# A decoder trunk in fp32r matmuls: rows of matmuls behind the last store, and the order in the last k tile

## The chip, the core and the metric

The kernel runs on one NeuronCore of a Trainium2 chip. The metric is device time in microseconds, from the first to the last instruction of one execution with what lies around it. Before the change two runs took 2795.05 and 2796.88 us (median 2795.97). The core has five engines with queues of their own: TensorE (PE; its weight loads are PEld), VectorE (DVE), ScalarE (ACT), GpSimd (POOL) and SyncE (SP), which issues most DMAs.

## The reference

256 tokens of width 2048 pass through two layers. Each layer is a token mixer and a SwiGLU feed-forward, each wrapped in RMS norms and a residual. The first mixer is HGRN2 beside Mamba-2, the second a causal Conformer convolution.

```
h = x
for layer in range(DEPTH):                       # 2
    u = rms_norm(h, mix_pre_g[layer])
    m = hgrn2_mamba2_mixer(u, ...) if layer % 2 == 0 else conformer_conv_module(u, ...)
    h = h + rms_norm(m, mix_post_g[layer])
    u = rms_norm(h, ffn_pre_g[layer])
    h = h + rms_norm(swiglu(u, w_gate, w_up, w_down), ffn_post_g[layer])
return h
```

All data are float32. Nearly all arithmetic lies in the products with weights (w_in, w_out, w1, w2, gate, up, down).

## The kernel before

Activations lie transposed: `h` is a tile of 128 partitions x 16 k tiles x 256 tokens. A product with weights is done in fp32r, the type in which TensorE takes a rounded float32. To keep accuracy each operand is split into a high part (rounded) and a low part (the rest), and three of the four products are summed: high x high, high x low and low x high.

`weights` (line 138) loads 4 k tiles of a block of 256 columns by a DMA of SyncE, ScalarE makes the high part (line 144), VectorE or GpSimd the low part (line 145). The result lies in one of 4 buffers `whl`. `gemm` (line 178) goes over k in steps of 4 tiles, over the blocks, over the two halves `f` of a block, and over the k tiles, and calls `mm` (line 151) for each. `mm` issues two matmuls: `main`, whose moving operand has 512 columns (high and low part of the activations, side by side), and `cross`, with 256 (low part of the weights times high part of the activations), which is added into the second half of the same PSUM bank. In the last k tile of a half block `cross` comes first:

```
steps = [(ps, *main, first, last), (ps[:, 256:512], *cross, False, False)]
for o, l, r, st, sp in (steps[::-1] if last else steps):
```

`evac` (line 242) then takes a block out of PSUM: ScalarE copies the second halves (line 248), VectorE adds the first halves (line 252). `mm_one` (line 159) does the same product in three matmuls of 256 columns; the last block of each `project` uses it (line 161). `dt_rows` (line 542) issues its pairs of 512 and 256 columns on lines of its own, 552 and 555. Column sums for the norms (`colsum`, line 259) are fp32 matmuls of one column, which stand as two rows each in the trace.

The order of the instructions on each engine is set by a scheduler that simulates the program; `urgent`, `first` and `soon` give priorities, and `pin` keeps an instruction in the order in which the code issues it. The order within a queue is fixed before the run; engines wait for each other by semaphores.

`run` (line 492) goes through mixer, feed-forward, Conformer, feed-forward. The last `residual` calls `output` (line 336): it multiplies the last projection by the norm's factor, adds it to `h` and stores `h` in blocks of two k tiles, on SyncE's or ScalarE's queue. For blocks 3 and 4 (`PEF`) TensorE adds (lines 345 and 375) and ScalarE copies the sum into `h` (line 377). The last store is block 4's, on ScalarE's queue. With it the program ends.

Of the kernel before, what the change touches and what calls it, by code (L numbers as in the profile page):

```python
# [11 lines left out]
F32R = mybir.dt.float32r  # L12
# [4 lines left out]
P = 128  # L17
# [5 lines left out]
CK = 4  # L23
# [41 lines left out]
class Trunk:  # L65
# [84 lines left out]

    def mm(self, ps, main, cross, first, last, pin=False):
        nc = self.nc
        steps = [(ps, *main, first, last), (ps[:, 256:512], *cross, False, False)]
        for o, l, r, st, sp in (steps[::-1] if last else steps):
            self.last = nc.tensor.matmul(o, lhsT=l, rhs=r, start=st, stop=sp, skip_group_check=True)  # L155
            if pin:
                self.pin(self.last)
# [334 lines left out]
    def run(self, parts):  # L492
        us = self.residual(None, None, "mix_pre" if parts[0] in "mc" else "ffn_pre", 16 * (parts[0] == "c"), parts[0] == "c")
        layer = 0
        for n, p in enumerate(parts):
            nxt = parts[n + 1:n + 2]
            if p == "m":
                ms, rp = self.mixer(us)
            elif p == "c":
                ms, rp = self.conformer(us)  # L500
            else:
                ms, rp = self.ffn(layer, us)
                layer += 1
            pre = {"": None, "f": "ffn_pre"}.get(nxt, "mix_pre")
            us = self.residual(ms, rp, pre, layer * KT, nxt == "c")

# [674 lines left out]
```

## Time and profile before

| | |
|---|---|
| median of two runs | 2795.97 us |
| profiled execution: time | 2796.62 us |
| profiled execution: span, first to last instruction | 2794.9 us |
| TensorE busy | 2722.8 us, 97% |
| weight loads (PEld) busy | 2378.2 us, 85% |
| VectorE / ScalarE / GpSimd busy | 64% / 53% / 17% |
| mean granted TensorE clock | 0.986 |
| chain that ended last | TensorE 66%, VectorE 7% |

Times in the views are microseconds from the start of the span. "Busy" of TensorE is modelled: matmuls overlap, so the busy time of one is longer than its distance to the next. The granted clock is a share of full speed, 1.00 being 2.4 GHz and 0.50 being 1.2 GHz. A few matmul records can be missing from a trace.

### The profile page before, as it was taken

The numbers are of one execution on the slowest core, as the hardware profiler recorded it, in microseconds if no ns is written. First come the engines' busy times: TensorE is split into PE (matmuls) and PEld (weight loads), VectorE is DVE, ScalarE is ACT, GpSimd is POOL, SyncE is SP. The second block draws the span as 40 slices with busy tenths as digits, with TensorE's granted clock in tenths as the row PEclk, the third lists the DMA queues.
The fourth block names the chain that finished last, engine by engine and source line by source line (L and its number), as shares of the span: only waits on it lengthen the run. The fifth ranks groups of instructions, "written<-read, shape, count | busy, mean of one in ns | idle before, by whom it ended". The sixth has DMA issues, their size and how long they took to land.

```text
span 2794.9 us, 41558 instructions
## 1 busy us (share of the span) xinstructions
PE 2722.8 (97%) x16362; PEld 2378.2 (85%) x16362; DVE 1786.4 (64%) x2372; ACT 1470.2 (53%) x1978; POOL 483.4 (17%) x308
## 2 busy tenths in 40 slices
PE   7999999999999999999999999999999999999998
PEld 6888888887788888888888888987878888888887
DVE  6876777887645655555544458996575555554444
ACT  6676775666544544444444445555554444444443
POOL 2221321111100100000000016981110000000001
PEclk9999999999999999999999999999999999999999
DMA  6454455555565555555566644542545555556663
GB/s 216 155 173 157 154 168 159 171 175 169 177 186 162 160 188 188 185 186 188 185 186 188 188 152 155 182 150 79 163 160 187 187 185 186 188 185 186 187 188 121
DMA packets 134020, 482.41 MB, mean 173 GB/s; under 512 B 14880, under 2 KB 15424, under 8 KB 133824
## 3 DMA queue, kind: packets, MB, share of 16 engines
q1 hardware_dynamic: 132528, 476.41, 54.6%
q8 instruction: 128, 2.10, 0.3%
q10 hardware_dynamic: 1296, 3.35, 0.3%
q14 instruction: 68, 0.56, 0.1%
HBM read 477.57 MB, written 2.13 MB: 172 GB/s over the span
## 4 chain that ended last, share of the span: by engine, by line
PE 66%; DVE 7%; issue 1%; ACT 1%; ACTq 0%; DVEq 0%
PE g L155 57%; PE g L161 7%; DVE pc L911 3%; DVE u L288 1%; DVE whl L145 1%; DVE m L426 0%; DVE h L429 0%; DVE ca L977 0%; PE ss L262 0%; ACT whl L144 0%; DVE m L351 0%; PE g L921 0%; DVE h L415 0%; PE pc L921 0%; PE rb L275 0%
## 5 line engine op out<-in xcount | busy, mean ns | idle before, releaser
L145 DVE TENSOR_TENSOR whl<-raw,whl 128x1024 fp32r<-128x1024 f32 x846 | 1060.3, 1255 | 902.1 <-ACT whl L144 896.3
L155 PE MATMUL g<-u,whl 128*128 128x256 f32 (+1 forms) x8448 | 1524.4, 342 | 28.5 <-DVE u L288 26.9
L144 ACT CAST whl<-raw 128x1024 fp32r<-128x1024 f32 x898 | 939.0, 1048 | 1086.0 <-PE g L155 869.4
L155 PEld LDWEIGHTS g<-u,whl 128*128 128x128 f32 x8448 | 1303.8, 190 | 234.6 <-DVE u L288 31.4
L155 PE MATMUL g<-hid,whl 128*128 128x512 f32 (+1 forms) x2464 | 434.7, 339 | 0.6 <-DVE m L252 0.6
L155 PEld LDWEIGHTS g<-hid,whl 128*128 128x128 f32 x2464 | 377.3, 188 | 57.9 <-PE g L155 1.1
L480 POOL TENSOR_TENSOR sg<-sg,rpre 128x512 f32<-128x512 f32 x44 | 77.6, 1763 | 874.9 <-ACT sg L479 874.9
L161 PE MATMUL g<-u,whl 128*128 128x256 f32 x1536 | 193.2, 289 | 9.2 <-DVE u L288 6.1
L161 PEld LDWEIGHTS g<-u,whl 128*128 128x128 f32 x1536 | 190.8, 197 | 11.1 <-DVE u L288 7.7
L911 DVE SCALAR_TENSOR_TENSOR pc<-ca,dw,pc 128x240 f32<-128x240 f32 (+29 forms) x414 | 158.2, 461 | 0.4
L311 POOL TENSOR_TENSOR acc<-acc,sq 128x512 f32<-128x512 f32 x24 | 37.9, 1579 | 645.1 <-ACT sq L310 645.1
L145 POOL TENSOR_TENSOR whl<-raw,whl 128x1024 fp32r<-128x1024 f32 x52 | 126.0, 2442 | 37.1 <-ACT whl L144 34.8
L155 PE MATMUL g<-whl,u 128*128 128x256 f32 (+1 forms) x512 | 95.8, 343 | 1.2 <-DVE f L252 1.2
L155 PEld LDWEIGHTS g<-whl,u 128*128 128x128 f32 x512 | 78.8, 188 | 13.3 <-issue 1.5
L155 PE MATMUL g<-cx,whl 128*128 128x512 f32 x448 | 84.3, 352 | 4.3 <-DVE cx L1060 2.8
L248 ACT COPY ev<-g 128x512 f32<-128x512 f32 x153 | 88.1, 576 | 0.0
L791 POOL TENSOR_TENSOR e<-e,cbm 128x384 f32<-128x384 f32 x32 | 45.6, 1444 | 235.6 <-ACT e L789 188.3
L155 PEld LDWEIGHTS g<-cx,whl 128*128 128x128 f32 x448 | 72.1, 198 | 16.5 <-DVE cx L1060 3.5
L155 PE MATMUL g<-mixb,whl 128*128 128x512 f32 (+1 forms) x448 | 81.1, 340 | 1.5 <-DVE mixb L132 1.5
L155 PE MATMUL g<-mixa,whl 128*128 128x512 f32 x448 | 80.3, 339 | 1.5 <-DVE m L252 1.5
L155 PEld LDWEIGHTS g<-mixb,whl 128*128 128x128 f32 x448 | 68.7, 188 | 12.6 <-DVE mixb L132 2.2
L155 PEld LDWEIGHTS g<-mixa,whl 128*128 128x128 f32 x448 | 68.9, 188 | 12.1 <-issue 2.1
(278 smaller groups left out, 1851.7 us busy)
## 6 DMA issues: line engine op xcount, KB each, us to landing
raw<-ffn_gu SPq DMA_DIRECT2D x352, 512.0 KB, 3.5
raw<-w_in SPq DMA_DIRECT2D x208, 512.0 KB, 4.5
raw<-ffn_d SPq DMA_DIRECT2D x176, 512.0 KB, 3.6
raw<-w SPq DMA_DIRECT2D x96, 512.0 KB, 3.6
raw<-w_out SPq DMA_DIRECT2D x64, 512.0 KB, 3.8
row<-csd SPq DMA_DIRECT2D x16, 256.0 KB, 5.6
h<-x ACTq DMA_DIRECT2D x4, 512.0 KB, 9.0
raw<-w_dt SPq DMA_DIRECT2D x2, 512.0 KB, 4.2
```

The lines of the kernel that those rows point to most:

```text
L144: nc.scalar.copy(hl[:, :n, 0], raw[:, :n])
L145: (lo or nc.vector).tensor_tensor(hl[:, :n, 1], raw[:, :n], hl[:, :n, 0].bitcast(F32), ALU.subtract)
L155: self.last = nc.tensor.matmul(o, lhsT=l, rhs=r, start=st, stop=sp, skip_group_check=True)
L161: self.last = self.nc.tensor.matmul(ps[f] if banks else ps[:, f], lhsT=hl[:, wi, f * P:(f + 1) * P], rhs=x[:, xi], start=k == 0 and n == 0 ...
L248: nc.scalar.copy(ev[:, sl], ps[:, sl, 256:512])
L288: pin(self.nc.vector.scalar_tensor_tensor(u[:, 1], x, sc, u[:, 0].bitcast(F32), op0=ALU.mult, op1=ALU.subtract))
L311: nc.gpsimd.tensor_tensor(acc, acc, sq, ALU.add)
L480: nc.gpsimd.tensor_tensor(sg, sg, self.bc2(r), ALU.mult)
L791: G.tensor_tensor(e, e, cb, ALU.mult)
L911: x = V.scalar_tensor_tensor(pc[f][:, s:T], a[:, f, 0:T - s], tap(2 * i + f, s), pc[f][:, s:T], op0=ALU.mult, op1=ALU.add)
```

## The change

It has two parts. In `mm` the last k tile now issues `main` first and `cross` second, as all others do; the flag that ends the accumulation moves to `cross`. Behind the last `residual` a new function `trials` is called. ScalarE copies parts of the final `h` into three `whl` buffers and eight activation tiles; the copies read blocks 4 to 7 of `h`. Then TensorE runs matmuls on these, all fp32r but for `tiny`, each with start and stop set, into two PSUM tiles that nothing reads: `pairs` as in `mm` (with other moving operands, other banks or other weights as options), `grouped` and `swapped` (the same pairs in other orders), `wide` (three of 512 columns with activations as the stationary operand), `ones` (256 columns), `halves` (512 columns) and single matmuls of 1 to 512 columns in between (`kick`, `tiny`). Three passes go through all forms, four passes through `pairs` behind kicks of each length.

```diff
@@ -150,8 +150,7 @@
 
     def mm(self, ps, main, cross, first, last, pin=False):
         nc = self.nc
-        steps = [(ps, *main, first, last), (ps[:, 256:512], *cross, False, False)]
-        for o, l, r, st, sp in (steps[::-1] if last else steps):
+        for o, l, r, st, sp in ((ps, *main, first, False), (ps[:, 256:512], *cross, False, last)):
             self.last = nc.tensor.matmul(o, lhsT=l, rhs=r, start=st, stop=sp, skip_group_check=True)
             if pin:
                 self.pin(self.last)
@@ -503,6 +502,127 @@
                 layer += 1
             pre = {"": None, "f": "ffn_pre"}.get(nxt, "mix_pre")
             us = self.residual(ms, rp, pre, layer * KT, nxt == "c")
+        self.trials()
+
+    def trials(self):
+        nc = self.nc
+        S = nc.scalar
+        flat = lambda a: a.rearrange("p a b -> p (a b)")
+        hw = self.h.rearrange("p a b -> p (a b)")
+        ws = []
+        for n in range(3):
+            w = self.whl.tile([P, CK, 2, 256], F32R, tag="whl", name=f"pw{n}")
+            wf = w.rearrange("p a b c -> p (a b c)")
+            self.pin(S.copy(wf, hw[:, 2048:4096]))
+            ws.append(w)
+        xs = []
+        for n in range(8):
+            x = self.A(F32R, name="px")
+            self.pin(S.copy(flat(x), hw[:, 3584 - 64 * n:4096 - 64 * n]))
+            xs.append(x)
+        xf = [flat(x) for x in xs]
+        ps = [self.ps_gemm() for _ in range(2)]
+        o = [p[:, j] for p in ps for j in range(2)]
+        st = {"k": 0}
+
+        def mm(out, l, r):
+            self.pin(nc.tensor.matmul(out, lhsT=l, rhs=r, start=True, stop=True, skip_group_check=True))
+
+        def places(n):
+            k0 = st["k"]
+            st["k"] += n
+            for j in range(k0, k0 + n):
+                i, f, t = j % 4, j // 4 % 2, j // 8 % 2
+                yield i, f, slice(f * P, (f + 1) * P), ws[t], j % 8
+
+        def pairs(n, gap=False, banks=False, other=False):
+            for i, f, s, w, k in places(n):
+                b = o[k % 4] if banks else o[f]
+                r = ws[2][:, 0:2, 0] if gap else xf[k]
+                lo = ws[2][:, i, 1, s] if other else w[:, i, 1, s]
+                mm(b, w[:, i, 0, s], r)
+                mm(b[:, 256:512], lo, ws[2][:, 0, 0] if gap else xs[k][:, 0])
+
+        def grouped(n, g):
+            pl = list(places(n))
+            for q in range(0, n, g):
+                for i, f, s, w, k in pl[q:q + g]:
+                    mm(o[f], w[:, i, 0, s], xf[k])
+                for i, f, s, w, k in pl[q:q + g]:
+                    mm(o[f][:, 256:512], w[:, i, 1, s], xs[k][:, 0])
+
+        def swapped(n):
+            for i, f, s, w, k in places(n):
+                m = [(o[f], w[:, i, 0, s], xf[k]), (o[f][:, 256:512], w[:, i, 1, s], xs[k][:, 0])]
+                for a in (m[::-1] if k % 2 else m):
+                    mm(*a)
+
+        def wide(n, gap=False, banks=False):
+            for i, f, s, w, k in places(n):
+                b = [o[(3 * k + j) % 4] for j in range(3)] if banks else [o[f]] * 3
+                hi = ws[2][:, 0:2, 0] if gap else flat(w[:, i])
+                lo = ws[2][:, 0:2, 1] if gap else flat(w[:, (i + 1) % 4])
+                mm(b[0], xs[k][:, 0, s], hi)
+                mm(b[1], xs[k][:, 0, s], lo)
+                mm(b[2], xs[k][:, 1, s], hi)
+
+        def ones(n, gap=False):
+            for i, f, s, w, k in places(n):
+                r = ws[2][:, 0:2, 0, 0:P] if gap else xs[k][:, 0]
+                mm(o[f][:, 0:256], w[:, i, 0, s], r)
+
+        def halves(n, gap=False):
+            for i, f, s, w, k in places(n):
+                mm(o[f], w[:, i, 0, s], ws[2][:, 0:2, 0] if gap else xf[k])
+
+        def kick(n):
+            mm(o[0][:, 0:n], ws[0][:, 0, 0, 0:P], xf[0][:, 0:n])
+
+        def tiny():
+            mm(o[0][:, 0:1], self.ident, self.ones[:, 0:1])
+
+        halves(24)
+        for _ in range(3):
+            pairs(16)
+            kick(128)
+            pairs(16, gap=True)
+            kick(384)
+            pairs(16, banks=True)
+            kick(256)
+            pairs(16, other=True)
+            tiny()
+            grouped(16, 2)
+            kick(128)
+            grouped(16, 4)
+            kick(320)
+            swapped(16)
+            kick(64)
+            wide(8)
+            kick(192)
+            wide(8, gap=True)
+            kick(448)
+            wide(8, banks=True)
+            kick(128)
+            ones(16, gap=True)
+            kick(256)
+            halves(16)
+            kick(192)
+            halves(16, gap=True)
+        for _ in range(4):
+            for n in (64, 128, 192, 256, 320, 384, 448, 512):
+                kick(n)
+                pairs(11)
+            kick(128)
+            kick(128)
+            pairs(11)
+            kick(256)
+            kick(256)
+            pairs(11)
+            kick(512)
+            kick(512)
+            pairs(11)
+            tiny()
+            pairs(11)
```

On TensorE, at the last k tile of a half block of the first products (`g` is the PSUM tile, `u` the activations, `whl` the weights). Before:

```order
L155 MATMUL g_195<-u_141,whl_325 128x512
L155 MATMUL g_195<-u_141,whl_325 128x256
L155 MATMUL g_195<-u_144,whl_325 128x256
L155 MATMUL g_195<-u_144,whl_325 128x512
L155 MATMUL g_195<-u_135,whl_325 128x512
L155 MATMUL g_195<-u_135,whl_325 128x256
```

And now:

```order
L154 MATMUL g_195<-u_141,whl_325 128x512
L154 MATMUL g_195<-u_141,whl_325 128x256
L154 MATMUL g_195<-u_144,whl_325 128x512
L154 MATMUL g_195<-u_144,whl_325 128x256
L154 MATMUL g_195<-u_135,whl_325 128x512
L154 MATMUL g_195<-u_135,whl_325 128x256
```

The two matmuls of the k tile `u_144` have changed places. There are 332 such places; one cast of ScalarE, one subtraction of GpSimd and a few matmuls near the norms also stand a place or two elsewhere.

On ScalarE, the end of the program as it is now (`out` and `h` are the output and the residual stream, `pw` and `px` the copies for `trials`):

```order
L357 DMA out<-h 128x512
L376 COPY h<-g_24318 128x512
L357 DMA out<-h 128x512
L516 CAST pw0_24351<-h_86 128x2048
L516 CAST pw1_24353<-h_86 128x2048
L516 CAST pw2_24355<-h_86 128x2048
L521 CAST px2994_24357<-h_86 128x512
L521 CAST px2995_24359<-h_86 128x512
```

Eleven copies stand behind the last store's issue, where the program ended before.

On TensorE, what stands behind the last matmul of `output` (line 374 now):

```order
L374 MATMUL g_24318<-m_23480,ident 128x512
L529 MATMUL g_24373<-px_24357,pw_24351 128x512
L529 MATMUL g_24373<-px_24359,pw_24351 128x512
L529 MATMUL g_24373<-px_24361,pw_24351 128x512
L529 MATMUL g_24373<-px_24363,pw_24351 128x512
L529 MATMUL g_24373<-px_24365,pw_24351 128x512
L529 MATMUL g_24373<-px_24367,pw_24351 128x512
L529 MATMUL g_24373<-px_24369,pw_24351 128x512
L529 MATMUL g_24373<-px_24371,pw_24351 128x512
```

These are the first eight of `halves(24)`; each waits for its own copy by ScalarE, the later ones for nothing but TensorE's own order.

## Rows read from the trace of the kernel before

**Rows 1.** The page's part 1: busy time, share of the span, instructions.

```profile
span 2794.9 us, 41558 instructions
PE 2722.8 (97%) x16362; PEld 2378.2 (85%) x16362; DVE 1786.4 (64%) x2372; ACT 1470.2 (53%) x1978; POOL 483.4 (17%) x308
```

**Rows 2.** Timeline of ScalarE's last instructions: start, us, engine, line, operation.

```profile
2791.35 0.59 ACT L377 COPY h<-g 128x512 f32<-128x512 f32 x1 [2.33 <-PE g L375]
2791.97 0.34 ACTq L358 DMA_DIRECT2D out<-h  x1
```

**Rows 3.** Stretches at the end: us, PE busy (matmuls), granted clock, DMA share, GB/s.

```profile
2786.00:2792.00 6.00, 4.11 (x4) 0.54 0.46 177
2792.00:2795.00 3.00, 0.00 (x0) 0.50 0.44 171
```

**Rows 4.** Timeline of TensorE in `dt_rows`: 16 pairs of 512 and 256 columns.

```profile
62.70 0.40 PE L552 MATMUL g<-u,whl 128*128 128x512 f32 x1
62.93 0.28 PE L555 MATMUL g<-u,whl 128*128 128x256 f32 x1
63.04 0.40 PE L552 MATMUL g<-u,whl 128*128 128x512 f32 x1
63.27 0.28 PE L555 MATMUL g<-u,whl 128*128 128x256 f32 x1
63.39 0.40 PE L552 MATMUL g<-u,whl 128*128 128x512 f32 x1
63.63 0.28 PE L555 MATMUL g<-u,whl 128*128 128x256 f32 x1
63.75 0.40 PE L552 MATMUL g<-u,whl 128*128 128x512 f32 x1
...
67.99 0.40 PE L552 MATMUL g<-u,whl 128*128 128x512 f32 x1
```

**Rows 5.** Dense stretches (columns as rows 3), and the timeline of the last one.

```profile
2200.00:2300.00 100.00, 100.00 (x568) 1.00 0.58 186
2754.00:2777.00 23.00, 23.00 (x193) 1.00 0.23 69
...
2753.84 23.64 PE L161 MATMUL g<-hid,whl 128*128 128x256 f32 x195
```

**Rows 6.** Timeline of TensorE at two calls of `colsum`, four matmuls.

```profile
2753.03 0.95 PE L262 MATMUL ss<-ones,acc 128*128 128x1 f32 x8
```

**Rows 7.** Groups of ScalarE by shape: count, busy us, mean ns, idle before.

```profile
L144 ACT CAST whl<-raw 128x1024 fp32r<-128x1024 f32 x898 | 939.0, 1048 | 1086.0 <-PE g L155 869.4 <-issue 135.6 <-PE g L161 54.6
L248 ACT COPY ev<-g 128x512 f32<-128x512 f32 x153 | 88.1, 576 | 0.0
```

**Rows 8.** Timeline of TensorE where it resumes behind idle times.

```profile
899.90 14.01 PE L155 MATMUL g<-u,whl 128*128 128x512 f32 x64 [2.98 <-DVE u L288]
...
920.10 10.89 PE L155 MATMUL g<-u,whl 128*128 128x512 f32 x44 [2.13 <-DVE u L288]
...
2038.36 8.35 PE L155 MATMUL g<-u,whl 128*128 128x512 f32 x35 [2.36 <-DVE u L288]
```

**Rows 9.** Stretches around these places, columns as in rows 3.

```profile
898.60:905.40 6.80, 5.50 (x17) 0.52 0.23 77
905.40:915.60 10.20, 8.52 (x48) 0.99 0.12 40
915.70:925.80 10.10, 7.71 (x21) 0.51 0.50 167
925.90:936.00 10.10, 10.10 (x62) 0.99 0.47 149
2035.20:2042.00 6.80, 4.43 (x12) 0.52 0.41 139
2042.00:2060.00 18.00, 17.72 (x105) 0.99 0.53 165
```

## The prediction

> **What bounds the kernel now.** I read the page's totals first: TensorE is busy 97% of a span of 2794.9 us [rows 1], so what is added to it, with nothing beside it that could shrink, is added to the time. The reader should then look at the tail, because the change puts its work there. The timeline ends with a copy of ScalarE from PSUM into `h` and the issue of the last store at 2791.97 us, done 0.34 us later [rows 2]; TensorE has nothing to do from there on, and the granted clock has fallen to 0.50, the 1.2 GHz level [rows 3]. The third reading is the price of the added instructions, from stages that run the same shapes in the same type (fp32r, 128 rows). The best is the stage of `dt_rows`, whose two matmuls stand on lines of their own, so that the timeline doesn't merge them [rows 4]. A "mean ns of one" is no price: matmuls overlap, so I take the distance from one start to the next.
>
> **The prices.** In [rows 4] the 512-column matmul starts at 62.70 and, fifteen pairs on, at 67.99: 5.29/15 = 0.353 us for a pair of 512 and 256 columns. The page of a long stage agrees: 568 matmuls in 100 us are 0.176 each [rows 5]. Within the pair, the 256 starts 0.23 to 0.24 after the 512 (mean 0.236) and the next 512 starts 0.11 to 0.12 after that. A run of 256-column matmuls alone, in the last block, takes 23.64/195 = 0.121 each [rows 5]. So a matmul costs 0.461 ns a column (0.236/512), and short ones don't fall below some floor: eight rows of one column take 0.95 us, 0.119 each [rows 6].
>
> **First part: trials().** Counting the calls gives 2208 matmuls of 871,751 columns:
> 864 pairs: seven lots of 16 (pairs four times, grouped twice, swapped) in each of 3 passes are 336; twelve lots of 11 in each of 4 passes are 528. At 0.353: 305.0 us.
> 336 matmuls of 512 columns that stand alone: 24 at the start, and in each of 3 passes 72 of `wide` and 32 of `halves`. At 0.236: 79.3 us. No row shows 512 behind 512 for long; pair minus 256 alone (0.353 - 0.121 = 0.232) says 78.0, so this is worth 1.3 us either way.
> 48 of 256 columns (`ones`): 48 x 0.121 = 5.8 us.
> 89 kicks: 51 of 256 columns and more, 18,816 columns in all, 8.7 us at 0.461 ns; 38 shorter ones at the floor of 0.119, 4.5 us.
> 7 times `tiny`, fp32 with one column, two rows in the trace each (four such matmuls of `colsum` show eight [rows 6]): 7 x 0.24 = 1.7 us.
> Sum: 305.0 + 79.3 + 5.8 + 8.7 + 4.5 + 1.7 = 405.0 us.
>
> The start is set by ScalarE, which must make the operands first. It is free at 2791.97 + 0.34 = 2792.3. Its copies take 0.576 us for 128x512 and 1.048 for 128x1024 [rows 7], so 0.472 more for each further 512: about 1.99 for 128x2048. Three of these are 5.97 us and eight of 128x512 are 4.61; with 0.03 between two of them the first `px` is there at 2799.0 and the last at 2803.2. The first eight matmuls wait for one `px` each and are shorter than its copy even at half clock (0.47), so they hide under it. The other 16 of the first 24 then run free. The clock is low when they begin. How long it stays low: TensorE starts again at 899.90, 920.10 and 2038.36 [rows 8] and the stretches at 0.5 end at 905.4, 925.8 and 2042.0 [rows 9], that is 3.6 to 5.7 us after the work came back. Counted from 2799.0, it rises between 2802.6 and 2804.7. I take 2804.5: 1.3 us at half clock does about 3 of the 16, the other 13 take 3.1 us, and the passes begin at 2803.2 + 4.4 = 2807.6. With all 16 cold it would be 3 us more, with none 0.6 less.
>
> What remains is the sum without the first 24 (5.7 us): 399.3. End: 2807.6 + 399.3 + 0.2 (a 256-column matmul lasts 0.28 us, 0.16 more than its step) = 3207.1. The last stores are long landed by then and hide. The profiled execution took 2796.62 for its span of 2794.9, so 1.7 lie around the span: 3208.8. Its time is 0.65 over the median of 2795.97 that the forecast is set against: **3208 us**.
>
> **Second part: the order in the last k tile.** 332 half blocks now issue 512, 256 where they issued 256, 512. The columns, the instructions and the waits' number are the same. Nobody waits for the middle of a half block: the copy out of PSUM waits for the last instruction, which is now the 256 one. Steps differ by at most 0.01 from one place to the next in [rows 4]; 332 x 0.01 bounds it at 3.3 us in either direction, and I take nothing. The other moves that the schedule shows (one cast of ScalarE and one subtraction of GpSimd a place later, two short matmuls of a norm earlier) neither add nor remove work; a late one of about 1 us each is their bound.
>
> **A rule against this sum.** Each 512 in [rows 4] takes 0.236 us, each 256 in [rows 5] 0.121, at granted clock 1.00. The Trainium skill, "TensorE: Matmul & The Clock Gate", section "Back-to-back issue gap", says that a warm stream needs N/2.4 + 2.5 ns for N columns, which would be 0.216 and 0.109. By that the whole sum is an estimate of 871,751/2400 + 2208 x 0.0025 = 369 us in place of 405; the rows are about a tenth dearer, and they decide the sum. It is a rival below.
>
> **Rivals.**
> (a) *Cheap trials.* The tenth above one column a tick (2.4 GHz: 512 columns 0.213) comes from something that the trials lack, such as the weights' transfers, the other engines' reads, or adding into PSUM (all trial matmuls overwrite). One column a tick is 871,751/2400 = 363 us, 42 less: 3166. By the rule of the Trainium skill named above it would be 3172. Against it: the last block's 256s step at 0.121 with DMA at 0.23 and most engines idle, the same as elsewhere [rows 5]. 7%.
> (b) *Some forms are dearer.* The "gap" lots read the moving operand in two runs of 256 that lie apart, which no matmul here does. Per pass they are 16 pairs, 24 + 16 of 512 and 16 of 256: 5.6 + 9.4 + 1.9 = 17.0 us, 51 in three passes. At double price the time is 3259; at a third more, 3225. Likewise `wide`, with 216 matmuls. 11%.
> (c) *The trials hardly run.* This one ends on the other side, not slower. No instruction reads the PSUM tiles that they write; if whatever turns the program into what the chip runs drops them, only the copies are left: 2803.8 + 1.7 = 2805, no change. It decides once fewer than some 250 of the 2208 remain, 250 x 0.18 us being 45 us beside the 9 of the copies. Against it: the built program's TensorE list holds them all, behind line 375's. 3%.
> (d) *The clock stays low* through the trials: twice 405, about 3610. In stages as dense as these it is 1.00 [rows 5]. 1%.
>
> **Chances and range.** The forecast's case has 78%. Its own unknowns are the price of a pair (1% is 4 us), the start (-0.6 to +3), the order (3) and the moved steps (2): 3197 to 3221. To hold 8 in 10 beside the rivals, and since some lots may each be a tenth off without being (a) or (b), I take 3183 to 3236. What a measurement here can tell from no change is 2%, 56 us: slower 97%, within 2% 2%, faster 1%, the last two from (c).
>
> **What would show it.** In the profile after: a span near 3207; the first trial matmul at 2799; the clock rising some 2 to 6 us later and staying at 1.00; stretches of `pairs` at 0.353 a pair whatever kick stands ahead; the same step of 0.23 to 0.24 in `wide` and `halves`; the main program's last store at 2792 within 5 us. Wrong would be: pairs at 0.32 (a); gap lots that take longer than their neighbours (b); no rows of the trials (c).

## The result, and the profile after

The changed kernel takes 3178.35 us (two runs, 3177.28 and 3179.42) against 2795.97: 1.1367 of the time before, 95% interval 1.1344 to 1.139. Slower, as forecast, but 4.7 us under the range and 30 under the number. The profiled execution took 3177.28 us for a span of 3175.6.

The end of the main program comes first. The timeline after, at the same instructions as [rows 2], and then the first of `trials` (start, us, engine, line, operation, idle before):

```profile
2766.91 0.59 ACT L376 COPY h<-g 128x512 f32<-128x512 f32 x1 [2.29 <-PE g L374]
2767.53 0.34 ACTq L357 DMA_DIRECT2D out<-h  x1
2767.96 5.50 ACT L516 CAST pw<-h 128x2048 fp32r<-128x2048 f32 x3 [0.47 <-ACT h L376]
2773.36 4.25 ACT L521 CAST px<-h 128x512 fp32r<-128x512 f32 x8
...
2774.03 13.63 PE L529 MATMUL g<-px,pw 128*128 128x512 f32 x57 [7.16 <-ACT px L521]
```

The last store is issued at 2767.53 where it was at 2791.97: the main program, whose instructions are the same but for 332 exchanged pairs, became 24.4 us shorter. Where that went shows in counts of matmuls per 100 us. After, columns as in [rows 3]:

```profile
1000.00:1100.00 100.00, 100.00 (x579) 1.00 0.61 190
1500.00:1600.00 100.00, 100.00 (x567) 1.00 0.63 185
2200.00:2300.00 100.00, 100.00 (x579) 1.00 0.62 190
2600.00:2700.00 100.00, 100.00 (x567) 1.00 0.63 187
```

Before, the stretch from 2200 held 568 [rows 5]. It lies in the second feed-forward's gate and up blocks, and now holds 579; the stretches from 1500 and 2600, in the down projections, hold 567, no more than before:

```profile
1500.00:1600.00 100.00, 100.00 (x568) 1.00 0.63 185
2600.00:2700.00 100.00, 100.00 (x571) 1.00 0.64 189
```

The same two speeds stand in `dt_rows`, now on lines 672 and 675:

```profile
61.03 0.39 PE L672 MATMUL g<-u,whl 128*128 128x512 f32 x1
61.26 0.28 PE L675 MATMUL g<-u,whl 128*128 128x256 f32 x1
61.38 0.39 PE L672 MATMUL g<-u,whl 128*128 128x512 f32 x1
61.61 0.28 PE L675 MATMUL g<-u,whl 128*128 128x256 f32 x1
...
66.23 0.39 PE L672 MATMUL g<-u,whl 128*128 128x512 f32 x1
```

From 61.03 to 66.23 are fifteen pairs: 0.3467 us each, where [rows 4] had 0.3527. The starts of all pairs in the trace say it to the nanosecond. A long stream of pairs runs in a **rhythm**. The slow one repeats every three pairs (steps of 233, 117, 241, 120, 236, 113 ns: 1060 for three, 353.3 a pair). The fast one takes 346.7 a pair (230 and 117, or 232, 118, 231, 112, 233, 117, 231, 113). Each gate and up stage has 1408 pairs; the last 1335 run on without a wait. Before, all but the first 20 or so of these were in the slow rhythm, some 1316 in either stage. After, all 1335 are in the fast one.

The page's totals after, beside [rows 1]:

```profile
span 3175.6 us, 46001 instructions
PE 3099.9 (98%) x18577; PEld 2723.7 (86%) x18577; DVE 1785.8 (56%) x2372; ACT 1483.5 (47%) x1989; POOL 483.4 (15%) x308
```

TensorE has 2215 rows more: the 2208 matmuls of `trials`, and a second row for each of the seven `tiny`.

### The profile page after: what moved, and what is told of

It is laid out like the page before. It is cut to its first block, busy times and chain, and to the rows that moved or that the text cites. A ratio compares the mean times of both kernels' runs of the same rounds, so it can differ in the third digit from the quotient of the medians.

```text
span 3175.6 us, 46001 instructions
## 1 busy us (share of the span) xinstructions
PE 3099.9 (98%) x18577; PEld 2723.7 (86%) x18577; DVE 1785.8 (56%) x2372; ACT 1483.5 (47%) x1989; POOL 483.4 (15%) x308
## 4 chain that ended last, share of the span: by engine, by line
PE 70%; DVE 6%; ACT 1%; issue 1%; ACTq 0%; DVEq 0%
PE g L154 50%; PE g L529 13%; PE g L160 6%; DVE pc L1031 2%; DVE u L287 1%; DVE whl L145 1%; DVE m L425 0%; DVE h L428 0%; DVE ca L1097 0%; PE ss L261 0%; ACT whl L144 0%; DVE m L350 0%; PE g L1041 0%; DVE h L414 0%; PE pc L1041 0%
## 5 line engine op out<-in xcount | busy, mean ns | idle before, releaser
L154 PE MATMUL g<-u,whl 128*128 128x512 f32 (+1 forms) x8448 | 1503.7, 339 | 27.4 <-DVE u L287 27.3
L529 PE MATMUL g<-px,pw 128*128 128x256 f32 (+3 forms) x1793 | 320.2, 339 | 7.2 <-ACT px L521 7.2
L529 PEld LDWEIGHTS g<-px,pw 128*128 128x128 f32 x1793 | 276.6, 189 | 49.3 <-ACT px L521 10.4
L154 PE MATMUL g<-whl,u 128*128 128x512 f32 (+1 forms) x512 | 95.2, 341 | 0.6 <-DVE f L251 0.6
L154 PE MATMUL g<-mixb,whl 128*128 128x512 f32 x448 | 81.7, 342 | 1.6 <-DVE mixb L132 1.6
```

The costliest lines, as they stand in the source:

```text
L529: self.pin(nc.tensor.matmul(out, lhsT=l, rhs=r, start=True, stop=True, skip_group_check=True))
```

## The experiments

Three theories of the 24.4 us were on the table. *Rhythm*: an exchange at a half block's end throws the stream into the slow rhythm, where it stays. *Local*: each reversed end costs 24.4/332 = 74 ns where it stands. *Schedule*: the code behind the last store moved the main program.

### One part at a time

e1_order_only has no `trials`; e2_trials_only has the old order. Their edits are the two halves of the change; e1_order_only's, against the changed kernel, is this line:

```diff
-        self.trials()
```

> The changed kernel without trials(): only the order in the last k tile differs from the kernel before. Three theories of where 24.4 us of the main program went. Rhythm: the pair stream of TensorE runs in one of several repeating rhythms, of 353.3 or 346.7 ns a pair, and the reversed half-block end throws it into the slow one; without it 2771.5 us. Local: each of the 332 reversed ends costs 74 ns where it stands; also 2771.5. Schedule: the code behind the store moved the main program's schedule, and the order is worth nothing; 2796.

> The old order in the last k tile, with trials() behind the last store. The trials and their copies took 407.9 us in the changed kernel (3178.35 - 2770.45 of e1_order_only). If the two parts of the change add up, this is the kernel before (2793.5 to 2796.0) and 408: 3201.5 to 3204, with gate and up pairs at 353.3 ns. If the trials' presence is what moved the main program, 3178.

Measured: e1_order_only 2770.45 us (2767.34 to 2770.68) against 2793.52 before it, ratio 0.9916 (0.9901 to 0.9931). e2_trials_only 3201.12 against 2795.35, 1.1452 (1.1419 to 1.1485). The parts add up: the order alone gives 23.1 us back, the trials alone cost 405.8. *Schedule* falls. In a stretch of the first gate and up stage, e1_order_only, then e2_trials_only:

```profile
1000.00:1100.00 100.00, 100.00 (x579) 1.00 0.53 190
```

```profile
1000.00:1100.00 100.00, 100.00 (x568) 1.00 0.60 187
```

The rate goes with the order, whatever stands behind the store.

### The order or the flag

e9_flag_on_main exchanges nothing but leaves the flag that ends the accumulation on the 512-column matmul.

```diff
-        for o, l, r, st, sp in ((ps, *main, first, False), (ps[:, 256:512], *cross, False, last)):
+        for o, l, r, st, sp in ((ps, *main, first, last), (ps[:, 256:512], *cross, False, False)):
```

> As e1_order_only (512 columns first, 256 second, everywhere), but the flag that ends the accumulation stays on the 512-column matmul, as it was before the change. If the order of the two matters: 2767 to 2778 and gate and up pairs at 346.7. If the place of the flag was what slowed the kernel before: 2796 and 353.3.

2774.42 us, 0.9931 (0.9913 to 0.9949); both gate and up stages are fast:

```profile
1000.00:1100.00 100.00, 100.00 (x579) 1.00 0.53 190
2200.00:2300.00 100.00, 100.00 (x579) 1.00 0.53 190
```

e1_again, the same order with the flag on the 256-column matmul, took 2773.92 beside it. The flag has no part in it.

### One place instead of 332

e3_one_block_reversed puts the old order back in one block of the first feed-forward:

```diff
+            self.flip = i == 1 and layer == 0
             ps = pss[0] if i == 0 else self.gemm(wgu, g[:1], us)[0]
+            self.flip = False
```

> As e1_order_only, but one block of 256 columns (i = 1, gate, first feed-forward) has the old reversed order in its two half-block ends. Rhythm: the two ends switch the stream to 353.3 ns a pair and it stays there for what is left of the gate and up blocks, 42 blocks x 32 pairs x 6.67 ns = 9.0 us over e1_order_only; the second feed-forward stays at 346.7. Local: 2 x 74 ns = 0.15 us over e1_order_only, and 346.7 in both.

2777.76 us, 7.3 over e1_order_only in the same batch (*rhythm* forecast 9.0). Times of whole programs vary by several us from one execution to the next, so the rates of the stages decide. The stretches of the first and of the second feed-forward:

```profile
1000.00:1100.00 100.00, 100.00 (x567) 1.00 0.52 187
2200.00:2300.00 100.00, 100.00 (x579) 1.00 0.53 190
```

Two exchanged places slow all 1485 pairs behind them, from 941 to 1466 us. *Local* allowed 0.15 us. The steps around the first of the two, from the starts in the trace (columns of the matmul: step to the next, ns):

```
... 512:230 256:117 512:230 256:116 | 256:119 512:232 | 512:231 256:113 512:233 256:117 512:241 256:120 ...
```

The two exchanged matmuls themselves cost 351 ns, as a pair should. Behind them the fast rhythm (230, 117) has become the slow one (233, 117, 241, 120).

The kernel before shows the same switch. The long runs of pairs of its two gate and up stages start fast and turn slow at their first exchanged places, at 944.38 and 2062.30 us, and the steps around the first of these are those shown above. So does its first down projection, at 1501.16, the first exchanged place behind the wait at 1472.

An exchange is not a one-way switch, though. In e2_trials_only, which has the old order, the first down projection is slow, turns fast at the exchange at 1499.76 us, and slow again at the one at 1530.29:

```profile
1471.00:1496.00 25.00, 25.00 (x143) 1.00 0.62 187
1502.00:1527.00 25.00, 25.00 (x146) 1.00 0.65 191
1533.00:1558.00 25.00, 25.00 (x143) 1.00 0.63 187
```

And where a second exchange stands four pairs behind one that led to the fast rhythm, the stream can stay fast (before, at 79.28 us, for one). In the two gate and up stages of before and of e2_trials_only no exchange leads back.

e7_one_end_and_reset is finer: one exchanged place in all, at i = 4, and four short matmuls at i = 13.

```diff
+                        if self.reset and k == 0 and f == 1:
+                            for _ in range(4):
+                                self.nc.tensor.matmul(ps[:, f, 0:1], lhsT=self.ident, rhs=self.ones[:, 0:1], ...)
...
+            self.flip = i == 4 and layer == 0
+            self.reset = i == (13 if layer == 0 else 4)
```

> As e1_order_only; in the first feed-forward one single half-block end is reversed (i = 4, gate, f = 0) and four 1-column fp32 matmuls (overwritten) stand between the half blocks of i = 13, gate; in the second feed-forward only the four matmuls stand, at i = 4. Rhythm: first feed-forward 346.7 ns a pair up to i = 4, 353.3 from there to i = 13, 346.7 behind it: 9 x 64 pairs x 6.67 ns = 3.8 us and 0.5 for the four matmuls; second feed-forward 346.7 throughout, 0.5 us more. Sum 4.8 over e1_order_only. Local: 0.07 + 1.0 us, 346.7 throughout.

Stretches before the exchange, behind it (two), behind the four matmuls, and in the second feed-forward:

```profile
950.00:1000.00 50.00, 50.00 (x291) 1.00 0.59 191
1050.00:1100.00 50.00, 50.00 (x284) 1.00 0.57 184
1150.00:1200.00 50.00, 50.00 (x285) 1.00 0.58 185
1250.00:1300.00 50.00, 50.00 (x290) 1.00 0.59 190
2200.00:2250.00 50.00, 50.00 (x290) 1.00 0.59 189
```

Fast, slow from 1012 to 1206 us (547 pairs), fast again, as *rhythm* said. From the first matmul of the stage's long run to its last, 2671 matmuls, the stream takes 467.5 us, where e1_order_only's takes 462.9: 4.6 more, forecast 4.3. The whole program took 2782.74, 12 us over e1_order_only and not 4.8 (they ran in different batches; the kernel before took 1.8 us more in this one). In the profiled executions, which lie 14.4 apart, 0.9 belong to the four matmuls of the second feed-forward, and the rest arose where nothing was edited: 4.3 us ahead of this stretch, 1.7 in the Conformer and the start of the second feed-forward, 2.9 in the second down projection, slow here and fast there. Which rhythm a stage falls into behind a wait is not fixed by the code: the changed kernel and e1_order_only have the same main program, and its second down projection holds 567 matmuls from 2600 to 2700 us there and 579 here:

```profile
2600.00:2700.00 100.00, 100.00 (x579) 1.00 0.59 190
```

### What switches it

e4_kick_64_and_192 puts one short matmul into each gate and up stage, e5_kick_192_in_projections 26 of them into the projections:

```diff
+                        if self.kick and k == 0 and f == 1:
+                            self.nc.tensor.matmul(ps[:, f, 0:self.kick], lhsT=main[0], rhs=main[1][:, 0:self.kick], ...)
```

> As e1_order_only, with one extra matmul in each feed-forward, between the half blocks of the block i = 1, gate: 64 columns in the first feed-forward, 192 in the second (written where the next matmul overwrites). Rhythm: in the trials a 64-column one was followed by 353.3 a pair and a 192-column one by 346.7, so the first feed-forward's gate and up blocks take 9.0 us more and the second's only the 0.1 us of the matmul itself. Local: 0.1 us more in each, 346.7 in both.

> As e1_order_only, with a 192-column matmul (overwritten) between the half blocks of each block's first k step in the projections (w_out, down, w2), 26 in all. There the stream of the changed kernel is in the slow rhythm in the two down projections (434 pairs each) and in w2 (154 pairs). Rhythm: these 1022 pairs go from 353.3 to 346.7, 6.8 us less, against 26 x 0.1 = 2.6 us for the matmuls: 4.2 us below e1_order_only, about 2767. Local: 2.6 us above it, about 2774.

e4: 2767.11, 2782.11 and 2778.68 us. In the profiled execution (the first) both stages are fast. That tells little of the kicks: the first stage was fast, turned slow behind the 64 columns as *rhythm* forecast, and fast again 1.5 us later behind short fp32 matmuls of the norm; the second was slow before and behind the 192 and fast behind the same short matmuls. In this execution every later stage is fast too, the first down projection among them, and it is the quickest seen of a program without trials (the other two executions left no trace, so their rhythms are not known):

```profile
1500.00:1600.00 100.00, 100.00 (x579) 1.00 0.60 190
2600.00:2700.00 100.00, 100.00 (x579) 1.00 0.59 190
```

e5: 2775.03 us, 4.6 over e1_order_only where *rhythm* had forecast 4.2 under it. In its profiled execution both down projections run fast, as forecast (580 and 581 matmuls in the stretches above), but they were so ahead of the first kick, and each kick cost 0.12 us where 0.1 was forecast. In this trace the kick chooses no rhythm, it leaves the one that is there: in the down projections steps like 230, 117, 88 (the kick), 257, 117, 235, 116, 230 leave the stream fast, in the long run of w_out (tile `mixa`) it stays slow. So 192 columns are not always followed by the fast rhythm, as they were in the trials. e6_lots_behind_kicks tested that at large, with lots of 12 pairs behind the last store:

```diff
+        steps = [tiny] + [lambda n=n: kick(n) for n in (64, 128, 192, 256, 512)]
+        for a in steps:
+            for b in steps:
+                a()
+                pairs(12)
+                b()
+                pairs(12)
```

> The changed kernel with other trials behind the last store: for every ordered choice of two out of tiny (1 column, fp32) and 64, 128, 192, 256, 512 columns, that matmul, 12 pairs, the other matmul, 12 pairs. Rhythm: each lot settles within a few pairs at 353.3 or 346.7 ns a pair. If a short matmul sets the rhythm alone, all lots behind the same one read the same; if it shifts what was there, the reading depends on the lot before. Local (no rhythm): all lots the same.

Of the 72 lots, 36 end at 353.3 ns a pair and 36 at 346.7 (mean of the pairs 6 to 11, from the starts in the trace), none between. No short matmul settles it alone. Number of lots that follow, by the rhythm before and behind:

| matmul | slow, slow | slow, fast | fast, slow | fast, fast |
|---|---|---|---|---|
| tiny | 2 | 2 | 3 | 4 |
| 64 | 1 | 6 | 1 | 4 |
| 128 | 0 | 7 | 5 | 0 |
| 192 | 6 | 0 | 4 | 2 |
| 256 | 4 | 2 | 0 | 6 |
| 512 | 3 | 2 | 6 | 1 |

(the first lot has none before it). 128 columns changed the rhythm in all 12 cases; behind the others it depends on more than the rhythm that was there. That a short matmul shifts the phase of the stream, and that the outcome hangs on the phase it met, fits these counts; the phase itself was not followed.

Four short fp32 matmuls had been followed by the fast rhythm in several places, and e8_reset_in_projections tried them as a cure, beside another batch of e1. Its premise, that this had always been so, does not hold: in e1_order_only's own trace the column sum at 2034.79 us is followed by 16 slow pairs (steps 232, 118, 241, 120, 236, 113), and the one at 932.60 in e7_one_end_and_reset likewise.

```diff
+                self.reset = g[0] == 2 and bias is None
                 pss = self.gemm(w, g, x, hook=hook if g[0] == 0 else None, K=K)
+                self.reset = False
```

> As e1_order_only, with four 1-column fp32 matmuls (overwritten) in three projections (w_out and the two down projections), between the half blocks of the first block behind the first PSUM wait. In the runs so far such a group, or a column sum of four, was followed by 346.7 ns a pair whatever stood before. Rhythm: the 314 + 434 + 434 pairs behind them run at 346.7 always; an execution of e1_order_only has some of them at 353.3, up to 7.9 us in all, and the matmuls cost 3 x 0.55 us: about 2767 in every execution, 2 to 3 us below e1_order_only. If the reset isn't one: 1.7 us above it.

> The kernel of e1_order_only once more, beside e8_reset_in_projections. Rhythm: 2767 to 2778, by how many of its projections happen to start in the slow rhythm.

e8: 2775.49 us (2773.72 to 2777.74); e1_again: 2773.92 (2772.77 to 2776.62), ratio to the kernel before 0.9930 (0.9916 to 0.9943). No gain: 1.6 us over it, as forecast for the case that the four matmuls don't reset (1.7). They didn't: in e8's profile the first stretch, behind those of w_out, is fast, the second, behind those of the first down projection, is slow:

```profile
765.00:790.00 25.00, 25.00 (x147) 1.00 0.63 191
1465.00:1490.00 25.00, 25.00 (x143) 1.00 0.58 190
```

So the best version found is the kernel without the trials and with the usual order: two batches at 0.9916 and 0.9930 of the time before.

## Why the prediction was wrong

Against its own working, all for the profiled execution (3208.8 forecast, 3177.28 measured):

**The second part failed.** The step reads: "Steps differ by at most 0.01 from one place to the next in [rows 4]; 332 x 0.01 bounds it at 3.3 us in either direction, and I take nothing." It priced the exchanged matmuls, and there it was right: they cost what a pair costs (351 ns in e3_one_block_reversed). What it left out is that the order sets how fast the *following* pairs run. Measured: -24.4 us at the last store, -23.1 with e1_order_only alone. The places of [rows 8] where the two gate and up stages get under way stand in the timeline after at:

```profile
895.26 13.82 PE L154 MATMUL g<-u,whl 128*128 128x512 f32 x64 [2.98 <-DVE u L287]
...
2023.13 8.14 PE L154 MATMUL g<-u,whl 128*128 128x512 f32 x34 [2.28 <-DVE u L287]
```

Against 899.90 and 2038.36 these are 4.6 and 15.2 us earlier, and the last store 24.4: 4.6 us came in the mixer, 10.6 with the first feed-forward and the Conformer, 9.2 with the second feed-forward. Of the mixer's 4.6, 0.6 lie ahead of the first matmul (11.29 us before, 10.67 after) and 1.5 in the long run of pairs of w_out, now fast; the rest is spread over many short runs of pairs. A gate and up stage alone is 1316 x 6.67 ns = 8.8 us. The down projections gave 0.4 us each: they were mostly slow before and are so after.

The profile of before held the clue. In [rows 4] the pairs start at 62.70, 63.04, 63.39 and 63.75: 0.34, 0.35 and 0.36, a pattern that I averaged away. So the price of 0.353 was that of the slow rhythm. And the same pairs run at another rate elsewhere. Before, in the first down projection:

```profile
1473.00:1498.00 25.00, 25.00 (x146) 1.00 0.63 186
1503.00:1528.00 25.00, 25.00 (x144) 1.00 0.64 189
```

Both are the same instructions of one stage. A price that has two values under the same conditions should have been followed to what lies between them: here the first exchanged place behind the wait at 1472 us, at 1501.16.

**The trials.** The mechanism was right, and their sum was within 2% (392.9 us for 399.5). They start 6.2 us behind the freed ScalarE (2767.87 to 2774.03), forecast 6.7: its copies of 128x2048 took 5.50/3 = 1.83 us, not 1.99. The clock rose between 3.7 and 4 us after the work came back, inside the 3.6 to 5.7 of the prediction, which had taken 5.5:

```profile
2774.00:2777.70 3.70, 3.67 (x7) 0.50 0.00 0
2777.70:2781.70 4.00, 4.00 (x18) 0.97 0.02 4
```

The passes begin at 2781.80, 13.9 us behind ScalarE's last store, forecast 15.3: -1.4 us. The passes take 392.9 us, forecast 399.5: -6.6. Pairs, kicks and `tiny`, which share their costs, take 303.5 + 11.2 + 1.0 = 315.6 for 319.9 (-4.3): the lots are slow or fast, 351.2 a pair on the mean. 512 columns alone (312 of them) take 71.4 for 73.6 (-2.3), 0.227 each once settled, not 0.236; the 48 of 256 take 5.9 for 5.8. The span ends 0.9 us behind the last matmul, which was not in the sum. In all -24.4 - 1.4 - 6.6 + 0.9 = -31.5 us.

The rivals: (b) didn't come. The three lots of `wide`, plain, gap and banks:

```profile
2821.88 5.72 PE L529 MATMUL g<-pw,px 128*128 128x512 f32 x24
...
2827.51 5.63 PE L529 MATMUL g<-pw,px 128*128 128x512 f32 x24
...
2833.18 5.62 PE L529 MATMUL g<-pw,px 128*128 128x512 f32 x24
```

A moving operand in two runs (the second row) costs no more, and no other bank (the third) makes it cheaper: 24 steady matmuls are 5.45 us with the last one's overhang taken off. The 5.72 of the first is the transition from the lot before. (a) has a grain of truth in that 512 alone went from 0.236 to 0.227, but 13.3 ns over the columns at 2.4 GHz (512: 213.3, 256: 106.7) stay on 512 and on 256 alike. The Trainium skill, "TensorE: Matmul & The Clock Gate", section "Back-to-back issue gap", gives 2.5 ns there, for what it calls the isolated gap of one matmul; the prediction put that as the need of a stream. The steady steps of 227 and 120 ns disagree, for fp32r with a new stationary operand each time. (c) and (d) didn't come: the trace has all rows of the trials, and the granted clock was 1.00 in the passes.

The range had no case in which the old program, with the same work, changes its speed.

**What stays open.** What in the chip makes the two rhythms, and why an exchange mostly leads from the fast one to the slow one and at some places back, isn't shown. The fast one is just the sum of the two steady steps, 226.7 + 120 = 346.7 ns; the slow one adds 20 ns in three pairs. Which rhythm follows a wait varied for one main program (567 and 579 matmuls in the second down projection, above). That the spread of one kernel's executions (e4: 2767.11 to 2782.11) comes of this is likely, but only one of them has a trace.

## What to carry to other kernels

Two orders of the same matmuls can differ in the time of everything behind them, not in their own: when an edit touches the order within a dense stream, compare matmuls per 100 us in the stages behind it, and don't bound it by the edited places. A stream that shows two rates for the same instructions within one profile has a state; find where it switches before pricing anything by its mean. An edit that looks like nothing beside a large one deserves its own run: here the small part was worth 23 us and the large part hid it.

## What the runs showed of the hardware

TensorE's stream of alternating 512- and 256-column fp32r matmuls, each with its own weights, has two stable rhythms, 353.3 and 346.7 ns a pair at granted clock 1.00. It kept either for over a thousand pairs until something disturbed it (1485 slow ones in e3_one_block_reversed, 1335 fast ones in the changed kernel). One exchanged pair can be enough: 547 slow pairs behind it in e7_one_end_and_reset. What a disturbance does is not fixed: an exchange also turned a slow stream fast (e2_trials_only, 1499.76 us), and of 72 lots behind short matmuls 36 were slow and 36 fast. Single shapes have one steady step in the trials: 227 ns for 512 columns, 120 for 256. A lone short matmul has most of its price in the next one: in e4_kick_64_and_192 the 64 columns step on after 29 ns, and the 512 behind them takes 313 where 230 is usual.
